# Writing a chunk mask into PSUM with VectorE instead of adding it with a TensorE matmul

## The chip, the cores and the metric

One Trainium2 chip, one of its cores. The metric is the device time of one execution, in microseconds (us).

## The reference

Two layers of a streaming encoder trunk over 1024 tokens of width 1024. Each layer norms its input, projects it, runs three branches (a gated linear recurrence, latent attention with 6 heads, a spatial gating MLP), and adds the normed output projection back. The change touches the scores of the attention alone. It is causal by chunks of 64 tokens: a query sees every key of its own chunk and of the chunks before it.

```python
s = jnp.einsum('bqhd,bkhd->bhqk', qb, k).astype(jnp.float32) * scale
mask = k_chunk[None, :] <= q_chunk[:, None]      # chunk = position // 64
s = jnp.where(mask[None, None], s, -jnp.inf)
p = jax.nn.softmax(s, axis=-1).astype(v.dtype)
return jnp.einsum('bhqk,bkhd->bqhd', p, v)
```

## The kernel before

All heavy products run on TensorE in a split form: each operand is kept as a rounded high part and a remainder, and `mm3` (L125 to L128) issues three matmuls for one product. The engines are written as one program; a scheduler orders each engine's instructions at build time from its own model of their durations, so a change in one operation can move others on every engine. At run time each engine executes its list in order, and a wait of one instruction holds all that stand behind it.

Each layer goes through these stages: the recurrent branch (`group`, `conv`, `lru_steps`), the spatial gating branch, the latents, the attention weights, the attention, and the output projection. The attention runs over 24 units per layer (6 heads x 4 pairs of 128-query blocks). For unit n the program emits `prepare(n + 4)` (queries and keys), `scores(n + 2)` and `mixv(n)`. So scores are made two units before they are used.

`scores` (from L884) makes two rows of scores per unit, one per 128-query block i, each over its (i + 1) x 128 keys. A row lies in PSUM in one of two buffers, `pw0` and `pw1`, each of two banks. The work of one row goes: `mm3` into the buffer, the mask, a row maximum on VectorE (L921), the exponential on ScalarE (L923, which also sums), a reciprocal on VectorE (L924), the scaling on GpSimd (L925). The buffer comes free when the exponential has read it. `mixv` then transposes the probabilities on TensorE (L945), splits them with ScalarE and VectorE or GpSimd (L365, L366), multiplies them with the values (L954), and combines the halves (L962, L963, L966).

The mask is needed in one 64x64 corner of a row: queries 0 to 63 of the block against keys 64 to 127 of the same block. Before the change the row's last `mm3` group is left open, and one more matmul closes it: `mask_a` (one partition, 128 columns, bf16: 64 ones, 64 zeros) times `mask_b` (one partition, 64 columns, bf16: -1e30). It adds -1e30 to the corner. The two tiles are set by three small memsets on VectorE at the start (L153 to L155). There are 2 layers x 24 units x 2 rows = 96 such matmuls, each with a weight load of its own.

At the program's start the prediction also speaks of `load_pre_gain` (L195, L197: a DMA, a transpose on TensorE), `load_x` (L183), the pre-norm (L327 on ScalarE, L133 to L142 and L338 on VectorE), the splitting of the transposed input (`turn_pair`, L349, L355, L356) and the convolution (L444 to L449), which reads the projected input out of `pw0` and `pw1`.

Of the kernel before, what the change touches and what calls it, by code (L numbers as in the profile page):

```python
# [9 lines left out]
BF16 = mybir.dt.bfloat16  # L10
# [9 lines left out]
EPS = 1e-6  # L20
# [17 lines left out]
NR, NF, NH = 33, 7, 3  # L38
# which of these run on VectorE rather than on GpSimd
W_ON_V = (C_U, C_GC)  # L40
Q_ON_V = ((0, 0), (0, 1), (1, 1), (4, 0))
Y_ON_V = (2, 4, 5, 6, 8, 9, 13, 14, 16, 19, 20, 21, 23)
WO_ON_V = (1, 4, 5)
# units of attention after which a token tile's share of the other branches is projected
EARLY = (20, 22)


class Slots:
    """A fixed set of buffers, handed out in the order in which they were given back."""

# [25 lines left out]
    def lend(self, t):  # L76
        """Add a buffer that is free for a while."""
        self.retired = [r for r in self.retired if r is not t]
        self.free_list.append(t)

    def retire(self, t):
        """No longer hand out a lent buffer."""
        self.retired.append(t)
        self.free_list = [r for r in self.free_list if r is not t]
# [5 lines left out]
def trunk_kernel(tc, A, out):  # L90
# [39 lines left out]
    def rsqrt(ms, n, out=None):  # L130
        """1 / sqrt(ms + EPS); times -8192 when `out` isn't given."""
        x, y, u = SM(n), SM(n), SM(n)
        V.tensor_scalar(out=x, in0=ms, scalar1=EPS, scalar2=None, op0=ALU.add)  # L133
        V.tensor_scalar(out=y.bitcast(I32), in0=x.bitcast(I32), scalar1=-0.5,
                        scalar2=float(0x5F3759DF), op0=ALU.mult, op1=ALU.add)
        for c in (3.0, 12.0, 768.0):
            if n == 1:
                V.scalar_tensor_tensor(out=u, in0=y, scalar=x, in1=y, op0=ALU.mult, op1=ALU.mult)  # L138
            else:
                V.tensor_tensor(out=u, in0=y, in1=y, op=ALU.mult)  # L140
                V.tensor_tensor(out=u, in0=u, in1=x, op=ALU.mult)
            V.scalar_tensor_tensor(out=y, in0=u, scalar=c, in1=y, op0=ALU.subtract, op1=ALU.mult)  # L142
        if out is not None:
            V.tensor_scalar(out=out, in0=y, scalar1=RSQ, scalar2=None, op0=ALU.mult)
        return y
# [4 lines left out]
    V.memset(ones, 1.0)  # L150
    mask_a = cst.tile([1, 128], BF16, name="mask_a")
    mask_b = cst.tile([1, 64], BF16, name="mask_b")
    V.memset(mask_a, 0.0)  # L153
    V.memset(mask_a[:, 0:64], 1.0)
    V.memset(mask_b, -1e30)  # L155
    Y = cst.tile([128, 8, T], F32, name="Y")
# [44 lines left out]
    def load_params():  # L201
        # per-channel parameters, transposed so that channels lie on partitions
        prow = HS.take((128, 128))
# [23 lines left out]
    def softplus_consts():  # L227
        V.tensor_scalar(out=hb, in0=par[:, 30:42], scalar1=0.5, scalar2=None, op0=ALU.mult)
        lam = par[:, 42:48]
        n = 6  # L230
        ab, kf, r, p, e, z, w = [SM(n) for _ in range(7)]
        # -|lam| = k ln2 + r
        V.tensor_scalar(out=ab, in0=lam, scalar1=-1.0, scalar2=None, op0=ALU.mult)
# [14 lines left out]
        V.tensor_tensor(out=e, in0=e, in1=p, op=ALU.mult)  # L248
        # log1p(e) = 2 atanh(e / (2 + e))
        V.tensor_scalar(out=z, in0=e, scalar1=2.0, scalar2=None, op0=ALU.add)  # L250
# [6 lines left out]
        V.scalar_tensor_tensor(out=p, in0=p, scalar=1.0, in1=z, op0=ALU.add, op1=ALU.mult)  # L257
        # softplus(-lam) = max(-lam, 0) + log1p(exp(-|lam|))
        V.tensor_scalar(out=k2, in0=lam, scalar1=-1.0, scalar2=0.0, op0=ALU.mult, op1=ALU.max)
# [58 lines left out]

    # ---------------------------------------------------------------- pieces
    def row_rsqrt(xs, cols=((0, 1024),), order=lambda i: i):  # L320
        """-8192 / rms of the rows of each of xs."""
        n = len(xs) * len(cols)
# [18 lines left out]
    def turn_pair(l, xn, hT, pair, slots):  # L341
        """Two token blocks of the normed input, turned and split in two parts."""
        half, o = pair // 2, (pair % 2) * 256
# [24 lines left out]
    class W:  # L368
        """Columns c0..c0+n of w_in, `per` row blocks to a buffer, split in two parts."""

# [28 lines left out]
    def feat(ps, hT, w, m, half, ts=slice(0, 512)):  # L399
        """[128 features, 512 tokens] of the input projection."""  # L400
        for k in range(8):
# [5 lines left out]
    def toks(hT, w, t, n, kind="P1"):  # L407
        """[128 tokens, n features] of the input projection."""
        ps = bank(kind)
# [7 lines left out]
    def gate_in(ps, yf, half):  # L417
        """Y[yf] = twice the silu of the projected gate."""
        th = HS.take((128, 512))
# [35 lines left out]
    def lru_steps(l, f, xc, gw):  # L455
        """The recurrence of channel block f as a list of pieces to emit."""
        c = l * 3 + f
# [62 lines left out]
    def stats(f0, n, ms, t0, width, eng, kind):  # L520
        """Mean square over n channel blocks for tokens t0..t0+512, onto partitions."""
        sq = []
# [14 lines left out]

    # ---------------------------------------------------------------- layers
    for r in yrow:
# [19 lines left out]
    for l in range(DEPTH):  # L559
        # ---- recurrent branch  # L560
        xc, last, gw = {}, [], []

        def group(g, half):
            pss = [bank("PF") for m in range(2)]
            if g == 0:
                # by pairs of token blocks, as they come
                for p in range(2):
# [46 lines left out]

        # ---- spatial gating branch
        for r in yrow[3:5]:
# [122 lines left out]

        # ---- latent attention: latents  # L740
        w = wl
# [49 lines left out]

        # ---- attention weights, norm gains folded in
        uqs, uq = [], []
# [30 lines left out]

        # ---- attention
        vs, vt, qs, kbs = {}, [], {}, {0: kb}
# [65 lines left out]
        def scores(h, j):  # L892
# [8 lines left out]
            for i in (2 * j, 2 * j + 1):  # L901
# [3 lines left out]
                ps = bank("P2") if j >= 2 else pw[:, (i % 2) * 512:(i % 2 + 1) * 512]  # L905
                # two equal pieces where the second would be too narrow for the full rate
                step = n // 2 if n == 640 else 512
                for c0 in range(0, n, step):
                    w = max(256, min(step, n - c0))
                    diag = c0 <= i * 128 < c0 + step  # L910
                    o0 = c0 // step * 512
                    mm3(ps[:, o0:o0 + w], sh, sl, kh[:, c0:c0 + w], kl[:, c0:c0 + w], True, not diag)
                    if diag:
                        d0 = o0 + i * 128 - c0 + 64
                        PE.matmul(ps[:, d0:d0 + 64], lhsT=mask_a, rhs=mask_b, start=False, stop=True)  # L915
                if step < 512:
# [16 lines left out]
        def mixv(h, j):  # L933
# [3 lines left out]
            for b0 in range(0, nb, 2):  # L937
                ps = bank("PT")
                pv = ps.rearrange("p (b q) -> p b q", b=2)
                end = b0 == nb - 2  # L940
                # the last key block comes first: the earlier query block doesn't see it
                for c, b in ((0, b0 + 1), (1, b0)):
# [92 lines left out]

        # ---- attention gate
        assert all(FS.idle(r) for r in yrow[5:])
# [38 lines left out]

        # ---- output projection, post-norm, residual, next pre-norm
        src = A["x"][0] if l == 0 else x1_dram
# [67 lines left out]
```

## Time and profile before

| what | value |
|---|---|
| time, median of 3 runs | 951.25 us (947.28 to 952.79) |
| span of the profiled execution | 948.6 us |
| TensorE (PE) busy | 899.4 us, 95% |
| VectorE (DVE) busy | 700.4 us, 74% |
| ScalarE (ACT) busy | 515.5 us, 54% |
| GpSimd (POOL) busy | 315.8 us, 33% |
| granted TensorE clock, mean | 0.984 of full |

The page gives no time of the profiled execution other than its span, from its first to its last instruction; this span lies inside the spread of the three times. The busy time of TensorE comes from modelled ends of pipelined matmuls; so for TensorE the distance from one matmul's start to the next one's tells more than the duration of one. The masks are issued in two stretches, from 252.4 to about 390 us in the first layer and from about 714 to 854.7 us in the second.

### The profile page before, as it was taken

The page shows a single profiled execution, that of the slowest core. Times are in us where ns is not written, and L with a number is a line of the kernel's source. Part 1 is how long each engine was busy: PE and PEld are TensorE (multiplying, and loading weights), DVE is VectorE, ACT ScalarE, POOL GpSimd, SP SyncE. Part 2 cuts the span into 40 slices and gives each one's busy share as a digit, 9 for nine tenths or more (in the row PEclk, how much of TensorE's full clock was granted, in tenths as well). Part 3 has the DMA queues.
Part 4 walks back from the last instruction along what each step waited for, and adds up shares of the span by engine and source line. Part 5 has one row for each costly group of instructions (what it writes and reads, how often), then busy time and mean ns, then how long its engine had stood idle before and what let it go on. Part 6 is the DMA issues. An engine that isn't in the chain of part 4 may idle for free. (4 is left out here: it accounts for less than half of the span.)

```text
span 948.6 us, 14005 instructions
## 1 busy us (share of the span) xinstructions
PE 899.4 (95%) x5078; PEld 775.8 (82%) x5078; DVE 700.4 (74%) x1645; ACT 515.5 (54%) x1026; POOL 315.8 (33%) x292
## 2 busy tenths in 40 slices
PE   4799999999999998998988999999999999899996
PEld 4698889998888877877887888899888888688785
DVE  6856976687588987588886498466857889857854
ACT  7346733346677886344444385323466778754312
POOL 2320013122156576353542000322103467655622
PEclk9899999999999999999999999999999999989999
DMA  7201410111000211022323032100100012201322
GB/s 269 52 24 44 120 31 1 41 39 32 1 1 23 89 45 45 26 86 98 122 92 97 1 114 65 38 18 23 48 1 1 1 46 67 67 23 46 123 99 89
DMA packets 35865, 53.39 MB, mean 56 GB/s; under 512 B 7800, under 2 KB 25812, under 8 KB 35796
## 3 DMA queue, kind: packets, MB, share of 16 engines
q1 hardware_dynamic: 35796, 52.50, 17.2%
q8 instruction: 40, 0.66, 0.3%
q14 instruction: 29, 0.24, 0.1%
HBM read 44.10 MB, written 8.39 MB: 55 GB/s over the span
## 5 line engine op out<-in xcount | busy, mean ns | idle before, releaser
L126 PE MATMUL pw<-R,R 128*128 128x512 f32 (+1 forms) x704 | 260.5, 371 | 13.8 <-ACT F L987 6.4
L127 PE MATMUL pw<-R,R 128*128 128x512 f32 (+1 forms) x704 | 253.3, 360 | 1.1 <-DVE R L356 1.1
L128 PE MATMUL pw<-R,R 128*128 128x512 f32 (+1 forms) x704 | 252.2, 359 | 0.7 <-POOL R L366 0.7
L126 PE MATMUL pa<-R,R 128*128 128x512 f32 (+3 forms) x540 | 188.6, 351 | 2.2 <-ACT F L768 2.2
L127 PE MATMUL pa<-R,R 128*128 128x512 f32 (+3 forms) x540 | 186.8, 346 | 0.0
L128 PE MATMUL pa<-R,R 128*128 128x512 f32 (+3 forms) x540 | 186.3, 346 | 0.0
L126 PEld LDWEIGHTS pw<-R,R 128*128 128x128 f32 x704 | 134.5, 191 | 34.3 <-ACT F L987 7.7
L128 PEld LDWEIGHTS pw<-R,R 128*128 128x128 f32 x704 | 134.2, 191 | 19.8 <-POOL R L366 1.1
L127 PEld LDWEIGHTS pw<-R,R 128*128 128x128 f32 x704 | 134.8, 192 | 18.6 <-DVE R L356 1.3
L385 POOL TENSOR_TENSOR R<-F,R 128x1024 fp32r<-128x1024 f32 (+1 forms) x22 | 49.3, 2256 | 190.8 <-ACT R L384 190.8
L925 POOL TENSOR_SCALAR F<-F,ring 128x128 f32<-128x128 f32 (+3 forms) x96 | 74.3, 776 | 114.6 <-DVE ring L924 109.2
L126 PEld LDWEIGHTS pa<-R,R 128*128 128x128 f32 x540 | 102.3, 190 | 12.3 <-ACT F L768 2.7
L128 PEld LDWEIGHTS pa<-R,R 128*128 128x128 f32 x540 | 102.3, 190 | 10.1
L127 PEld LDWEIGHTS pa<-R,R 128*128 128x128 f32 x540 | 102.4, 190 | 8.8
L921 DVE TENSOR_REDUCE ring<-pw 128x1 f32<-128x128 f32 (+3 forms) x96 | 71.9, 751 | 21.4 <-PE pw L915 20.4
L366 DVE TENSOR_TENSOR R<-pa,R 128x512 fp32r<-128x512 f32 (+1 forms) x120 | 73.8, 630 | 12.4 <-ACT R L365 11.4
L954 PE MATMUL pa<-R,R 128*128 128x256 f32 x480 | 77.9, 300 | 4.7 <-DVE H L963 4.5
L365 ACT ACTIVATE R<-pa 128x512 fp32r<-128x512 f32 (+1 forms) x120 | 64.4, 554 | 31.2 <-PE pa L945 25.3
L923 ACT ACTIVATE F<-pw,ring 128x128 f32<-128x128 f32 (+3 forms) x96 | 71.0, 740 | 13.9 <-DVE ring L921 13.2
L954 PEld LDWEIGHTS pa<-R,R 128*128 128x128 f32 x480 | 65.2, 195 | 7.8 <-DVE H L963 4.7
L945 PE MATMUL pa<-ident,F 128*128 128x128 f32 x432 | 67.4, 282 | 2.5 <-POOL R L366 1.5
L327 ACT ACTIVATE H<-F 128x1024 bf16<-128x1024 f32 (+2 forms) x33 | 31.4, 953 | 69.8 <-DVE F L1099 31.7
(276 smaller groups left out, 1400.3 us busy)
## 6 DMA issues: line engine op xcount, KB each, us to landing
F<-in_w_in SPq DMA_DIRECT2D x24, 512.0 KB, 3.8
F<-in_w_out SPq DMA_DIRECT2D x16, 512.0 KB, 3.6
F<-in_x SPq DMA_DIRECT2D x13, 512.0 KB, 3.5
F<-x SPq DMA_DIRECT2D x8, 512.0 KB, 4.3
x<-F SPq DMA_DIRECT2D x7, 512.0 KB, 3.0
out_y<-F SPq DMA_DIRECT2D x7, 512.0 KB
Y<-in_w_in SPq DMA_DIRECT2D x6, 512.0 KB, 3.5
F<-in_w_in SPq DMA_DIRECT2D x6, 352.0 KB, 3.0
```

Source lines behind the costliest of these rows:

```text
L126: PE.matmul(ps, lhsT=sh, rhs=mh, start=start, stop=False)
L127: PE.matmul(ps, lhsT=sh, rhs=ml, start=False, stop=False)
L128: PE.matmul(ps, lhsT=sl, rhs=mh, start=False, stop=stop)
L327: order(S_.activation(q.bitcast(BF16)[:, c], xs[i % len(xs)].rearrange("p a b -> p (a b)")[:, c], AF.Square, scale=1.0 / 32, accum_out=ms[ ...
L365: S_.activation(h, src, AF.Copy)
L366: (eng or G).tensor_tensor(out=lo, in0=src, in1=h.bitcast(F32), op=ALU.subtract)
L385: self.eng.tensor_tensor(out=lo, in0=st, in1=h.bitcast(F32), op=ALU.subtract)
L921: V.tensor_reduce(out=mx, in_=sv, axis=AX.XY, op=ALU.max, negate=True)
L923: S_.activation(p[:, 0:n].rearrange("p (a b) -> p a b", a=sv.shape[1]), sv, AF.Exp, bias=mx, accum_out=sm)
L925: G.tensor_scalar(out=p[:, 0:n], in0=p[:, 0:n], scalar1=rs, scalar2=1.0, op0=ALU.mult, op1=ALU.mult)
L945: PE.transpose(pv[:, c, i * 128:(i + 1) * 128], p[i][:, b * 128:(b + 1) * 128], ident)
L954: PE.matmul(o, lhsT=sv, rhs=pt[:, part, c * 256:(c + 1) * 256], start=(b == 0 and part == 0), stop=(b == nb - 1 and part == 1))
```

## The change

The mask tiles and their memsets go. The row's last `mm3` group closes itself, and VectorE writes -1e30 over the corner, 64 partitions by 64 columns of PSUM, before it takes the row maximum. The corner's scores are overwritten where they were added to. The program also loses its comments and docstrings. In the changed file the lines up to L150 keep their numbers, and those behind lie 5 lower, so the memset is L910 and the row maximum L916.

```diff
-    mask_a = cst.tile([1, 128], BF16, name="mask_a")
-    mask_b = cst.tile([1, 64], BF16, name="mask_b")
-    V.memset(mask_a, 0.0)
-    V.memset(mask_a[:, 0:64], 1.0)
-    V.memset(mask_b, -1e30)
...
                     w = max(256, min(step, n - c0))
-                    diag = c0 <= i * 128 < c0 + step
                     o0 = c0 // step * 512
-                    mm3(ps[:, o0:o0 + w], sh, sl, kh[:, c0:c0 + w], kl[:, c0:c0 + w], True, not diag)
-                    if diag:
+                    mm3(ps[:, o0:o0 + w], sh, sl, kh[:, c0:c0 + w], kl[:, c0:c0 + w], True, True)
+                    if c0 <= i * 128 < c0 + step:
+
                         d0 = o0 + i * 128 - c0 + 64
-                        PE.matmul(ps[:, d0:d0 + 64], lhsT=mask_a, rhs=mask_b, start=False, stop=True)
+                        V.memset(ps[0:64, d0:d0 + 64], -1e30)
```

The scheduler then orders the program anew. The lists differ in the two attention stretches and their surroundings and in the first 60 us or so; three places matter below. Names in the rows: `pw` and `pa` are PSUM tiles, F, H, R, Y and ring are SBUF tiles, and the number behind a name tells tiles apart (SBUF numbers are 5 lower after the change).

VectorE's list in the first layer's attention, before:

```order
L921 TENSOR_REDUCE ring<-pw_63 128x1
L366 TENSOR_TENSOR R_126<-pa_66,R_126 128x384
L366 TENSOR_TENSOR R_125<-pa_65,R_125 128x512
L963 SCALAR_TENSOR_TENSOR H_143<-pa_68,H_143 64x256
L881 TENSOR_TENSOR H_141<-pa_67,MQ 128x512
L924 RECIPROCAL ring<-ring 128x1 x2
L921 TENSOR_REDUCE ring<-pw_64 128x1
L366 TENSOR_TENSOR R_103<-F_138,R_105 128x1024
```

and after:

```order
L910 MEMSET pw_63 64x64
L958 SCALAR_TENSOR_TENSOR H_138<-pa_68,H_138 64x256
L876 TENSOR_TENSOR H_136<-pa_67,MQ 128x512
L361 TENSOR_TENSOR R_98<-F_133,R_100 128x1024
L916 TENSOR_REDUCE ring<-pw_63 128x1
L919 RECIPROCAL ring<-ring 128x1
```

The row maximum of the same row stood ahead of L963 (`mixv`), L881 (`queries`) and the 1024-wide remainder L366; now the memset stands ahead of these three and the maximum behind them. Over the whole list 27 of the 96 memsets have the maximum right behind them, 39 have one instruction between, 16 two and 14 three.

VectorE's list near 36 us, where the convolution reads the first projected blocks out of `pw0_63` and `pw1_64`, before:

```order
L449 SCALAR_TENSOR_TENSOR Y_82<-pw0_63,par_84,Y_82 128x510
L244 SCALAR_TENSOR_TENSOR ring_69<-ring_69 128x6
L446 COPY tails_99<-pw1_64 128x3
L449 SCALAR_TENSOR_TENSOR Y_82<-pw1_64,par_84,Y_82 128x511
L449 SCALAR_TENSOR_TENSOR Y_82<-pw0_63,par_84,Y_82 128x509
L245 TENSOR_SCALAR ring_69<-ring_69 128x6
L356 SCALAR_TENSOR_TENSOR R17_118<-pa2_67,pg_90,R16_117 128x256
L356 SCALAR_TENSOR_TENSOR R19_120<-pa3_68,pg_90,R18_119 128x256
```

and after:

```order
L444 SCALAR_TENSOR_TENSOR Y_77<-pw1_64,par_79,Y_77 128x511
L444 SCALAR_TENSOR_TENSOR Y_77<-pw0_63,par_79,Y_77 128x510
L239 SCALAR_TENSOR_TENSOR ring_69<-ring_69 128x6
L351 SCALAR_TENSOR_TENSOR R17_113<-pa2_67,pg_85,R16_112 128x256
L351 SCALAR_TENSOR_TENSOR R19_115<-pa3_68,pg_85,R18_114 128x256
L444 SCALAR_TENSOR_TENSOR Y_77<-pw1_64,par_79,Y_77 128x510
L351 SCALAR_TENSOR_TENSOR R21_117<-pa0_65,pg_85,R20_116 128x256
L351 SCALAR_TENSOR_TENSOR R23_119<-pa1_66,pg_85,R22_118 128x256
L444 SCALAR_TENSOR_TENSOR Y_77<-pw0_63,par_79,Y_77 128x509
L240 TENSOR_SCALAR ring_69<-ring_69 128x6
```

The last read of `pw0` (the 509-wide one) stood ahead of the four remainders of `turn_pair` and of the 510-wide read of `pw1`; now it stands behind these five. In both lists TensorE's next matmul writes `pw0`.

The queue of DMA issues (SP) at the program's start, before:

```order
L183 DMA F_134<-in_x 128x1024
L183 DMA F_135<-in_x 128x1024
L195 DMA H_141<-in_pre_norm_g 16x128
L375 DMA F_136<-in_w_in 128x4x256
L375 DMA F_137<-in_w_in 128x4x256
```

and after:

```order
L178 DMA F_129<-in_x 128x1024
L190 DMA H_136<-in_pre_norm_g 16x128
L178 DMA F_130<-in_x 128x1024
L370 DMA F_131<-in_w_in 128x4x256
L370 DMA F_132<-in_w_in 128x4x256
```

The load of the pre-norm gains and the load of the second token block have changed places.

## Rows read from the trace of the kernel before

**Rows 1.** The page, busy time of an engine, its share of the span and its instructions.
```profile
PE 899.4 (95%) x5078; PEld 775.8 (82%) x5078; DVE 700.4 (74%) x1645; ACT 515.5 (54%) x1026; POOL 315.8 (33%) x292
```

**Rows 2.** Busy time of each engine in stretches of the two attention stages. Columns: stretch, its length, then for PE, PEld (weight loads), DVE, ACT and POOL the busy us and the instructions, the granted TensorE clock, DMA share, GB/s.
```profile
240.00:260.00 20.00, 20.00 (x100) 16.66 (x99) 12.69 (x32) 11.51 (x30) 2.38 (x6) 1.00 0.00 1
260.00:360.00 100.00, 98.27 (x623) 81.39 (x622) 86.94 (x175) 79.15 (x172) 61.53 (x75) 1.00 0.13 43
360.00:400.00 40.00, 37.36 (x210) 32.18 (x210) 25.20 (x52) 20.46 (x40) 17.45 (x21) 0.96 0.08 27
700.00:720.00 20.00, 20.00 (x92) 16.42 (x91) 8.79 (x17) 12.57 (x20) 1.53 (x4) 1.00 0.00 0
720.00:820.00 100.00, 99.87 (x628) 83.47 (x627) 86.32 (x181) 78.16 (x176) 57.88 (x74) 1.00 0.11 38
820.00:860.00 40.00, 36.42 (x203) 30.87 (x202) 26.85 (x50) 23.48 (x48) 21.66 (x24) 0.91 0.08 27
```

**Rows 3.** The same view of shorter stretches: the one in which VectorE is fullest, and one behind a stall of TensorE.
```profile
320.00:340.00 20.00, 19.87 (x124) 16.17 (x123) 18.76 (x36) 18.66 (x38) 14.64 (x15) 1.00 0.24 80
...
364.60:368.00 3.40, 3.40 (x16) 3.21 (x15) 2.16 (x6) 2.25 (x5) 3.40 (x4) 0.50 0.02 5
```

**Rows 4.** The same view of the mask matmul's line (L915) alone, stretches as in rows 2; columns: stretch, length, PE busy (count), PEld busy (count), clock, DMA share, GB/s.
```profile
240.00:260.00 20.00, 0.99 (x5) 0.46 (x5) 1.00 0.00 1
260.00:360.00 100.00, 7.72 (x39) 3.53 (x39) 1.00 0.13 43
360.00:400.00 40.00, 0.79 (x4) 0.36 (x4) 0.96 0.08 27
700.00:720.00 20.00, 0.40 (x2) 0.18 (x2) 1.00 0.00 0
720.00:820.00 100.00, 7.72 (x39) 3.54 (x39) 1.00 0.11 38
820.00:860.00 40.00, 1.39 (x7) 0.64 (x7) 0.91 0.08 27
```

**Rows 5.** TensorE in order of time around two masks of the first layer. Columns: start (us), duration (us), engine, line, operation, tiles, array size, shape, count.
```profile
342.17 0.27 PE L127 MATMUL pw<-R,R 128*128 128x256 f32 x1
342.28 0.28 PE L128 MATMUL pw<-R,R 128*128 128x256 f32 x1
342.50 0.20 PE L915 MATMUL pw<-mask_b,mask_a 1*128 1x64 bf16 x1
342.62 0.50 PE L126 MATMUL pa<-R,R 128*128 128x512 f32 x1
342.96 0.40 PE L127 MATMUL pa<-R,R 128*128 128x512 f32 x1
343.19 0.39 PE L128 MATMUL pa<-R,R 128*128 128x512 f32 x1
...
349.59 0.40 PE L128 MATMUL pw<-R,R 128*128 128x512 f32 x1
349.92 0.20 PE L915 MATMUL pw<-mask_b,mask_a 1*128 1x64 bf16 x1
350.05 0.33 PE L945 MATMUL pa<-ident,F 128*128 128x128 f32 x1
```

**Rows 6.** Who waited for whom, longest first: for the first row TensorE from 250 to 360 us, for the others VectorE from 260 to 360 us and from 720 to 820 us. Columns: waiter, releaser, us in total, times, longest us.
```profile
PE pw L126 <- ACT F L923: 0.5, 1, 0.5
...
DVE ring L921 <- PE pw L915: 4.4, 9, 1.5
...
DVE ring L921 <- PE pw L915: 6.0, 12, 1.5
```

**Rows 7.** VectorE, operations near to the new one: a 64-column memset in SBUF and two small operations of which the second needs the first (in order of time), and the row maximum over 128 columns of PSUM (a group: count, busy us, mean ns, idle before it).
```profile
0.84 0.11 DVE L153 MEMSET mask_a<- 1x64 uint32 x1
...
7.49 0.17 DVE L133 TENSOR_SCALAR ring<-ring 128x2 f32<-128x2 f32 x1 [1.00 <-ACT H L327]
7.70 0.17 DVE L134 TENSOR_SCALAR ring<-ring 128x2 int32<-128x2 int32 x1
...
L921 DVE TENSOR_REDUCE ring<-pw 128x1 f32<-128x128 f32 x12 | 3.4, 282 | 2.9 <-PE pw L915 2.7
```

**Rows 8.** Groups of VectorE by line and shape: the three operations that now stand between a memset and its row maximum at the place shown.
```profile
L963 DVE SCALAR_TENSOR_TENSOR H<-pa,H 64x256 f32<-64x256 f32 x48 | 20.1, 419 | 10.2 <-ACT H L962 9.2
L881 DVE TENSOR_TENSOR H<-pa,MQ 128x512 f32<-128x512 f32 x24 | 16.4, 685 | 4.5 <-PE pa L879 3.3 <-POOL F L925 0.6 <-issue 0.2
L366 DVE TENSOR_TENSOR R<-F,R 128x1024 fp32r<-128x1024 f32 x7 | 9.3, 1324 | 5.1 <-PE pw L127 3.4 <-PE pa L128 1.5
```

**Rows 9.** The start, in order of time: the issue of the gains' load, the second square of the pre-norm, the five operations of VectorE near 40 us, and TensorE's first matmul behind them.
```profile
1.65 0.42 SPq L195 DMA_DIRECT2D H<-in_pre_norm_g  x1
...
6.31 1.06 ACT L327 ACTIVATE H<-F 128x1024 bf16<-128x1024 f32 x1 [0.94 <-PE pa L197]
...
39.28 0.87 DVE L356 SCALAR_TENSOR_TENSOR R<-pa,pg,R 128x256 fp32r<-128x256 f32 x2
40.07 0.74 DVE L449 SCALAR_TENSOR_TENSOR Y<-pw,par,Y 128x510 f32<-128x510 f32 x1
40.72 0.86 DVE L356 SCALAR_TENSOR_TENSOR R<-pa,pg,R 128x256 fp32r<-128x256 f32 x2
...
39.44 0.77 PE L126 MATMUL pw<-R,R 128*128 128x512 f32 x1 [6.14 <-DVE ring L245]
```

## The prediction, made before the changed kernel ran

> **What bounds the kernel now.** I read the share of busy time first, then the same busy times by stretches, because a share over the whole span mixes stages. TensorE is busy 95% of the span, VectorE 74% [rows 1]. In the two dense stretches of the attention, 260 to 360 us and 720 to 820 us, TensorE is busy 98.27 and 99.87 of 100 us, at a granted clock of 1.00 (2.4 GHz), and VectorE 86.94 and 86.32 [rows 2]. A busy TensorE need not be a limiting one, so I looked at who waits: TensorE waits 0.5 us in all for a score buffer [rows 6], and the only large wait of VectorE is for the mask matmul, 4.4 and 6.0 us [rows 6]. So the dense stretches run at TensorE's pace, with VectorE close behind: in its fullest 20 us it is busy 18.76, or 0.94 [rows 3]. The whole prediction rests on this narrow distance. TensorE loses work and VectorE gains some, so the second engine may take over before the first has given all its time back.
>
> **The change part by part.**
>
> *Mask matmuls removed.* There are 96: 39 in each dense stretch, 5 and 2 ahead of them, 4 and 7 behind [rows 4]. Their own 0.20 us in the records is not their price; I take the distance between starts with and without one. In the first example the 256-wide L128 starts at 342.28 and the second 512-wide matmul behind the mask at 342.96, so 0.68 us. Without a mask a 256-wide step takes 0.11 (342.17 to 342.28) and a 512-wide one 0.23 (342.96 to 343.19), together 0.34. The mask costs 0.34 us here [rows 5]: half ahead of its own start or in it, the rest in a slow first matmul behind it. In the second example 0.46 us pass from the 512-wide L128 to the first transpose, where 0.23 would do; the mask costs 0.23 [rows 5]. I take the middle, 0.29 us: 27.8 us in all, 11.3 in each dense stretch. The ends are 22 and 33 us.
>
> The Trainium skill ("TensorE: Matmul & The Clock Gate", Back-to-back issue gap) gives a matmul of up to 64 columns about 60 cycles, 25 ns. By it the 96 masks are worth 2.4 us, and the change next to nothing. The trace disagrees: even from the mask's start to the next start there are 0.12 us.
>
> *Memsets added.* 96 on VectorE, 64 columns, to PSUM. No row shows this. From below: the memset of 64 columns to SBUF takes 0.11 us [rows 7]. From above: a row maximum over 128 columns read from PSUM takes 0.28 us [rows 7], with twice the columns and a read. The maximum must wait for the memset's result; in the chain of small operations a needed result adds 0.04 us (0.17 us long, the next starts 0.21 later [rows 7]). I take 0.11 + 0.04 = 0.15 us, near the memset row because nothing is read. Its wait for TensorE is the one that the row maximum had, so it is not a new one. The ends are 0.11 and 0.28.
>
> The Trainium skill ("VectorE: DVE Perf Modes", The TRN2 errata) gives an operation that reads PSUM 120 cycles and one per column at 0.96 GHz; for 64 columns that is 0.19 us, an estimate from that page. With it the dense stretches would gain some 3.4 us less than in my sum, 944 us in all. No row here shows a write to PSUM by VectorE.
>
> *The balance in the dense stretches.* TensorE would need 100 - 11.3 = 88.7 us. VectorE would need 86.94 + 39 x 0.15 = 92.8 and 86.32 + 5.9 = 92.2, so VectorE ends last. It cannot be busy all the time while it works hand in hand with three engines. I take a share of 0.97, between the 0.94 that it has shown while it did not set the pace and 1.00. The stretches become 95.7 and 95.0 us, a gain of 4.3 and 5.0. At 0.94 the gain is 1.3 and 1.9, at 1.00 it is 7.2 and 7.8.
>
> *The edges.* From 240 to 260 and from 700 to 720 us VectorE is busy 12.69 and 8.79 of 20 us [rows 2], so the 7 masks there give back their whole price, 2.0 us. From 360 to 400 and 820 to 860 us TensorE already idles 2.6 and 3.6 us at the end of the softmax chain, and the clock sits partly at 0.50 (1.2 GHz) behind a stall [rows 2, 3]; of 11 masks worth 3.2 us I count 1.0. Both ends there, 0 and 3.2, lie inside the range.
>
> *The start.* The scheduler moved two things there that have nothing to do with masks. TensorE stood idle 6.14 us until VectorE had read `pw0` for the last time, and went on at 39.44 [rows 9]. That read now has five more operations ahead of it. They took 0.79 (39.28 to 40.07), 0.65 (40.07 to 40.72) and again 0.79 us [rows 9]: 2.2 us later, all of it on the path, since TensorE is the busy one from there to the attention. Against it, the gains' load is issued one place earlier, 0.42 us [rows 9]; the second square of the pre-norm waited for the transpose of these gains [rows 9], and the chain to the first matmuls starts from it. I count -0.4 us; if the token block, now issued later, decides there instead, +0.4. The three mask memsets at the start cost nothing: VectorE waits for that square anyway. Together +1.8 us.
>
> *Sum.* Gains 4.3 + 5.0 + 2.0 + 1.0 = 12.3, less 1.8: 10.5 us. The profiled execution spans 948.6 us, 2.6 below the median of the runs and inside their spread. I take the gain off the median: 951.25 - 10.5 = 940.8, say **941 us**. With the memset at 0.11 or the share at 1.00 it would be 937 or 935; at 0.28 about 951, at 0.94 about 947.
>
> **The rivals.**
>
> *TensorE keeps the pace.* The scheduler may pack VectorE's list so that its load does not matter; many of its operations overlap the tail of the one before, and the other waits of VectorE are short. Then all of 27.8 us comes back: 951.25 - 27.8 + 1.8 = 925 us (920 to 931 with the ends of the price). Against it stands the 0.94 in rows 3, where ScalarE too is busy 18.66 of 20.
>
> *VectorE takes up everything.* With 0.28 us a memset VectorE needs 97.9 and 97.2 us, at 0.97 that is the old 100; only the edges gain, and the start takes that back: about 951 us, no change.
>
> *The mask was never worth more than its issue slot.* If the slow matmul behind it has another cause and the 0.12 us overlap what follows, TensorE is hardly relieved: between 949 and 953 us. That is what the skill's rule on the issue gap above comes to. Both examples in rows 5 speak against it.
>
> *Score buffers held longer, and the kernel slower.* The order shows a memset, then `mixv`'s combine, a query product and a 1024-wide remainder, then the row maximum. These three take 0.42 + 0.69 + 1.32 = 2.4 us [rows 8], by which that row's exponential comes later and its PSUM buffer comes free later. In 30 of the 96 rows two or three operations stand between. TensorE needs one of the two buffers for every row, and its list cannot pass a matmul that waits. Net of the start my sum holds 10.5 us; that is gone if each of the 30 rows holds TensorE by 0.35 us, a seventh of the 2.4. At 0.6 us each it is 18 us lost against 10.5 won: 959 us. For it: VectorE has no room to catch up, and a stall of TensorE is followed by a stretch at clock 0.50 [rows 3]. Against it: today TensorE waits only 0.5 us for a buffer [rows 6], and scores are made two units ahead.
>
> **How the numbers follow.** A measurement of this kernel can tell about 0.5% (4.8 us) from no change, so faster means below 946.5 and slower above 956. My forecast, VectorE taking over part of the way, has 0.45 (931 to 946 us). TensorE keeping the pace has 0.14, VectorE taking up everything 0.21, the cheap mask 0.04, held buffers 0.16. Faster: 0.45 + 0.14 = 0.59. Same: 0.25. Slower: 0.16. The range goes from 926, which leaves out half of the second case, to 958, which leaves out the greater part of the last.
>
> **What would show it.** Right: no L915 matmul and the first matmul behind a score row at its plain step; dense stretches of some 95 us with VectorE at 0.95 or more; TensorE now with scattered waits for VectorE or ScalarE; memset rows of 0.11 to 0.2 us; TensorE starting on the second group near 41.5 us instead of 39.44. The forecast is wrong if VectorE's share stays near 0.87 while the stretch shrinks by 11 us (the first rival), if memsets take 0.28 us or more with what waits behind them (the second), if the matmuls at the place of the mask move up by 0.1 us or less (the third), or if TensorE's waits for ScalarE's exponential (now 0.5 us) grow to 10 us and more (the last).

## The result, and the profile after

The changed kernel takes 961.73 us (median of 4 runs, 960.38 to 965.3) against 949.9 of the kernel before on the same chip: ratio 1.0126, interval 1.0093 to 1.0158. It is 1.3% slower where 1% faster was forecast, and 3.7 us outside the range. The profiled execution is the longest of the four (span 963.5 us). One of e2's five executions below took 4226.61 us at a mean clock of 0.197 and is left out of its time.

The page's busy line, to be read beside [rows 1]: TensorE has 12 us less to do, VectorE 17 more, and the span is 15 longer.

```profile
PE 887.0 (92%) x4982; PEld 775.8 (81%) x4982; DVE 717.0 (74%) x1738; ACT 515.1 (53%) x1026; POOL 311.5 (32%) x292
```

The stretches of [rows 2], columns as there:

```profile
240.00:260.00 20.00, 20.00 (x94) 16.96 (x93) 9.91 (x20) 12.38 (x21) 0.94 (x3) 1.00 0.00 0
260.00:360.00 100.00, 93.35 (x581) 80.77 (x579) 93.45 (x216) 76.26 (x173) 55.62 (x73) 0.98 0.12 38
360.00:400.00 40.00, 34.17 (x188) 30.00 (x186) 26.97 (x56) 24.73 (x50) 23.06 (x25) 0.91 0.08 27
720.00:820.00 100.00, 93.76 (x573) 81.59 (x572) 90.56 (x213) 75.36 (x171) 51.05 (x70) 0.98 0.09 27
```

Without its 39 masks TensorE issued 584 matmuls from 260 to 360 us before; now it issues 581, and 573 instead of 589 in the second stretch (the stretches lie some 6 and 9 us earlier in the program now). So the freed time brought no more work through there. VectorE stands at 0.93 and 0.91, neither engine is full.

Who kept TensorE waiting (waiter, releaser, us in total, times, longest us; whole span, changed kernel):

```profile
PE pa L344 <- DVE F L333: 12.0, 2, 11.5
PE pa L940 <- DVE R L361: 11.5, 10, 2.8
PE pw L126 <- DVE ring L240: 9.9, 1, 9.9
PE pw L126 <- ACT F L982: 9.2, 4, 5.2
...
PE pw L126 <- ACT F L918: 3.2, 9, 0.5
```

The same waits in the kernel before:

```profile
PE pa L349 <- DVE F L338: 6.8, 3, 4.2
PE pw L126 <- ACT F L987: 6.4, 4, 2.9
PE pw L126 <- DVE ring L245: 6.1, 1, 6.1
...
PE pa L945 <- DVE R L366: 1.0, 1, 1.0
```

The wait for the exponential (L918), on which my slower case rested, is 3.2 us in all (0.5 before). What has grown are the waits of the transposes (L940) for VectorE's remainders, the two at the start (the first transposes, L344, and the second group, L126 behind L240), and the longest one for the projection's copy on ScalarE (L982). The memset's group (count, busy us, mean ns, idle ahead of it; who released VectorE) shows 0.112 us:

```profile
L910 DVE MEMSET pw<- 64x64 f32 x96 | 10.7, 112 | 9.2 <-PE pw L128 8.2
```

The start, answering to [rows 9]. The second square waits for the token block now (1.6 us later), two of VectorE's small operations take 2.3 us each, beside two splits on GpSimd, and the second group starts at 45.95 us instead of 39.44:

```profile
7.88 1.06 ACT L322 ACTIVATE H<-F 128x1024 bf16<-128x1024 f32 x1 [2.65 <-DMA F<-in_x]
...
10.38 4.65 POOL L380 TENSOR_TENSOR R<-F,R 128x1024 fp32r<-128x1024 f32 x2 [9.07 <-ACT R L379]
10.45 2.29 DVE L142 SCALAR_TENSOR_TENSOR ring<-ring 128x2 f32<-128x2 f32 x1
12.78 2.27 DVE L140 TENSOR_TENSOR ring<-ring 128x2 f32<-128x2 f32 x1
...
45.95 0.76 PE L126 MATMUL pw<-R,R 128*128 128x512 f32 x1 [9.87 <-DVE ring L240]
```

To find the place of a loss I took landmarks from the timelines (the first, 9th and last of the 48 row maxima of a layer, the last value product of `mixv`, the last matmul of `stats`). Lengths in us; e1, e3 and e10 are explained below:

| from - to | before | after | e1 | e3 | e10 |
|---|---|---|---|---|---|
| start - first row maximum, layer 0 | 252.7 | 258.7 | 255.4 | 255.5 | 255.3 |
| - 9th row maximum | 16.2 | 17.0 | 16.2 | 17.0 | 15.9 |
| - last row maximum | 119.2 | 116.2 | 118.1 | 114.9 | 112.2 |
| - last `mixv` product | 17.4 | 22.8 | 17.0 | 22.8 | 17.2 |
| - first row maximum, layer 1 | 308.8 | 309.2 | 307.3 | 307.9 | 307.0 |
| - 9th row maximum | 21.5 | 19.9 | 20.0 | 19.9 | 19.2 |
| - last row maximum | 119.2 | 115.9 | 116.5 | 116.1 | 113.7 |
| - last `mixv` product | 22.7 | 26.9 | 22.4 | 26.9 | 22.6 |
| - last `stats` matmul | 10.9 | 18.3 | 10.9 | 18.5 | 10.8 |
| - end | 60.0 | 58.6 | 59.9 | 58.6 | 60.0 |

The dense part between the 9th and the last row maximum is 3 us shorter per layer, which looks like the forecast. It isn't: in the changed kernel TensorE issues 67 instead of 50 `mm3` matmuls of the output projection behind the last row maximum (91 instead of 74 in layer 1), 17 x 0.23 = 3.9 us of work that was only moved there. The loss is 6.0 us ahead of the attention and, net of that moved work, in its tails and behind them (against e1 the dense part of layer 1 loses too, see e8).

### The profile page after: what moved, and what is told of

The parts are those of the page before. It is cut to its first block, busy times and chain, and to the rows that moved or that the text cites. A ratio compares the mean times of both kernels' runs of the same rounds, so it can differ in the third digit from the quotient of the medians.

```text
span 963.5 us, 13911 instructions
## 1 busy us (share of the span) xinstructions
PE 887.0 (92%) x4982; PEld 775.8 (81%) x4982; DVE 717.0 (74%) x1738; ACT 515.1 (53%) x1026; POOL 311.5 (32%) x292
## 3 DMA queue, kind: packets, MB, share of 16 engines
q1 hardware_dynamic: 35796, 52.50, 17.2%
## 5 line engine op out<-in xcount | busy, mean ns | idle before, releaser
L126 PE MATMUL pw<-R,R 128*128 128x512 f32 (+1 forms) x704 | 260.6, 372 | 23.4 <-DVE ring L240 9.9
L126 PE MATMUL pa<-R,R 128*128 128x512 f32 (+3 forms) x540 | 187.1, 349 | 2.2 <-ACT F L763 2.2
L126 PEld LDWEIGHTS pw<-R,R 128*128 128x128 f32 x704 | 135.2, 193 | 49.4 <-ACT F L982 10.5
L126 PEld LDWEIGHTS pa<-R,R 128*128 128x128 f32 x540 | 102.3, 190 | 11.8 <-ACT F L763 2.7
L918 ACT ACTIVATE F<-pw,ring 128x128 f32<-128x128 f32 (+3 forms) x96 | 71.0, 741 | 27.4 <-DVE ring L916 19.8
L940 PE MATMUL pa<-ident,F 128*128 128x128 f32 x432 | 67.8, 282 | 13.0 <-DVE R L361 11.5
L916 DVE TENSOR_REDUCE ring<-pw 128x1 f32<-128x128 f32 (+3 forms) x96 | 71.7, 749 | 1.3
L360 ACT ACTIVATE R<-pa 128x512 fp32r<-128x512 f32 (+1 forms) x120 | 62.3, 553 | 16.8 <-PE pa L940 14.1
```

Of the source, the lines that this page charges most:

```text
L126: PE.matmul(ps, lhsT=sh, rhs=mh, start=start, stop=False)
L360: S_.activation(h, src, AF.Copy)
L916: V.tensor_reduce(out=mx, in_=sv, axis=AX.XY, op=ALU.max, negate=True)
L918: S_.activation(p[:, 0:n].rearrange("p (a b) -> p a b", a=sv.shape[1]), sv, AF.Exp, bias=mx, accum_out=sm)
L940: PE.transpose(pv[:, c, i * 128:(i + 1) * 128], p[i][:, b * 128:(b + 1) * 128], ident)
```

## The experiments

**The tool: order held fast.** The change did two things, an operation and a new order. To have one without the other I wrote each engine's list into the kernel as a permutation and gave each instruction an edge behind its predecessor, which orders the issue and is meant to add no wait:

```diff
+def pin(tc):
...
+    for e, s in PIN.items():
+        at = np.frombuffer(zlib.decompress(base64.b85decode(s)), np.uint16)
+        for a, b in zip(at[:-1], at[1:]):
+            tc.add_manual_dep(by[e][b], by[e][a].name, mybir.DependencyInfo(
+                mybir.DependencyClass.NoSync, mybir.DependencyReason.DATA), reason="pin")
...
+    pin(tc)
```

Its 24 lines stand ahead, so in e1 and e3 line numbers are 24 above those of the changed kernel: `mm3` is L150 to L152, the projection's copy L1006, the one-column steps of the norm L162 and L166. The lists of the two kernels differ in three blocks (start, attention of layer 0, attention of layer 1 with its tail) and agree between them, so blocks can be mixed. All but the last experiment were timed in 5 rounds beside the kernel before (its medians 950.9 to 951.8). The kernel before with its own order held was not run; e11, which is that with 96 more matmuls, lies 1.0 us above it, so the holding itself changes little.

**e1: the memset, in the order of before.** Edit: changed kernel, `PIN` = order of before.

> The memset as in the change, but every engine's instructions pinned to the order of the kernel before (each memset directly ahead of its row maximum on VectorE, the mask matmuls simply missing on TensorE). Theory O (the change lost its time by the new order, at the start and in the attention): faster than before, 938 to 946 us, first group's second half at 39 to 41 us as before. Rival V (the memset itself costs it, because VectorE sets the attention's pace and every 0.11 us there delays a row maximum): no faster than before, 950 to 956 us.

945.53 us, ratio 0.994 (0.9918 to 0.9963). Theory O: the operation alone makes the kernel 5.5 us *faster*.

**e2: the matmul, in the new order.** Edit: kernel before, `PIN` = order of the changed kernel, the three small memsets later on VectorE.

> The converse: the mask matmul of the kernel before, but all other instructions pinned to the order of the changed kernel. Theory O: at least as slow as the changed kernel, 960 to 975 us, since order and matmuls both cost. Rival V: only the start's 6 us are lost, 954 to 958 us.

974.8 us (four executions), ratio 1.025 (1.0222 to 1.0277). The order costs about 24 us where nothing else is changed.

**e3: the changed kernel with the old start.**

> The changed kernel with its own order, only the start (TensorE's first 192, VectorE's first 136, ScalarE's first 46 instructions, SP's queue) pinned to the order of before. If the later start is a matter of order alone: the row maxima of layer 0 begin at about 252.7 us instead of 258.7, and the time falls by 5 to 7 us to 954 to 957 us. Rival (the start is late for what stands in the instruction stream, not for its order, or the lateness is absorbed later): less than 2 us gained, 960 to 963 us.

959.63 us, ratio 1.0091 (1.0071 to 1.011): 2.1 us better than the change, between what I expected and the rival, and the two intervals overlap. The row maxima begin at 255.5 us, not at 252.7, mostly because the two long rows stay (see e6, e17). Against e1 only the order of the two attentions differs: 14.1 us.

**e4: no mask at all, order of before.** Edit: the memset and its condition out.

> Neither matmul nor memset: the mask is left out of the computation, all else in the order of before. This shows what the 96 matmuls alone are worth where nothing takes their place. Theory O with VectorE near its limit: 930 to 941 us. If TensorE's time in the attention is fully covered by VectorE and the row maxima: 947 to 951 us. If all 27.8 us come back: 922 to 926 us.

932.71 us, ratio 0.9808 (0.9784 to 0.9833). So the 96 matmuls are worth 18.3 us, 0.19 each, and the memsets in their place cost 12.8 (e1 less e4), 0.13 each. The dense stretches of e1, then of e4 (columns as in [rows 2]):

```profile
260.00:360.00 100.00, 92.82 (x592) 80.46 (x591) 95.10 (x221) 80.26 (x177) 61.41 (x77) 1.00 0.14 43
720.00:820.00 100.00, 94.35 (x605) 82.39 (x604) 95.73 (x230) 81.60 (x184) 61.02 (x76) 1.00 0.14 43
```

```profile
260.00:360.00 100.00, 93.27 (x605) 82.38 (x604) 94.08 (x189) 83.85 (x182) 65.14 (x80) 0.99 0.13 43
715.00:815.00 100.00, 93.49 (x612) 83.12 (x611) 94.00 (x195) 85.47 (x190) 63.74 (x79) 1.00 0.14 43
```

VectorE at 0.95 and 0.96 in e1, as forecast, and matmuls brought through: 592 and 605 in e1 against 584 and 589 before, 605 and 612 with no mask.

**e6: do the dead memsets at the start matter?** Edit: e1 with the two mask tiles and their three memsets back.

> As e1 (memset, order of before), with the three small memsets of the two mask tiles kept at the places at the start where they stood before, though nothing reads the tiles now. Two VectorE rows of 2.2 us stood behind the first pre-norm in the kernel before and in front of it in e1. Theory S (what stands ahead in VectorE's stream sets where these long rows fall): first transposes at about 10.5 us instead of 15.3, second half of the first group near 39.4 instead of 41.7, time 942 to 944 us. Rival (they fall by something else): first transposes stay at 15, time 945 to 947 us.

944.62 us (0.9911 to 0.9946); transposes at 15.0 us. Theory S falls.

**e7: new order in layer 0 alone.**

> As e1, but the attention of layer 0 alone in the order of the changed kernel. Against e1 the new order cost 3 us by the end of layer 0's attention and 11 more in layer 1 (e3). Theory O: 948 to 950 us, all of it in place at layer 1's first row maximum. Rival (the order of layer 0 triggers the loss of layer 1, through buffers and queues left in another state): 954 to 960 us.

947.52 us (0.995 to 0.9986), 2.0 above e1, just under what O expected and with overlapping intervals; in the profile 3.8 us behind e1 at layer 1's first row maximum and 3.5 at the end. The loss stays in its layer, as O has it.

**e8: new order, tail of before.** Edit: from TensorE's instruction 4421, VectorE's 1504, ScalarE's 772, GpSimd's 260 on, the order of before.

> As e3 (memset, new order in both attentions, old start), but from about 840 us on, the tail of layer 1's attention, every engine in the order of before. Theory T (the new order's tail leaves TensorE without work for the 5.2 us in which ScalarE's projection copy waits, and the clock falls behind it): that gap shrinks to about 1.3 us, no 0.5 clock there, 951 to 954 us. Rival (the gap comes from the later arrival of the whole attention, not from the order in the tail): 957 to 960 us.

955.3 us (1.0031 to 1.0061), 4.3 us better than e3. The mechanism is T's, the size is half. The tail of layer 1 in e3, in order of time: a tile's norm runs on VectorE in one-column operations (L162, L166), which take 0.8 to 1.5 us while GpSimd runs eight splits (L385), where they take 0.16 to 0.22 us with GpSimd idle (897.4 to 898.4 us). Then the residual (L1118) frees the buffer that ScalarE's copy (L1006) takes next, by the program (the copy starts 0.09 us behind it in both kernels; the view names no releaser), and that copy frees TensorE's:

```profile
880.04 11.50 POOL L385 TENSOR_TENSOR R<-Y,R 128x640 fp32r<-128x640 f32 x8 [2.17 <-PE pa L973]
...
882.64 1.50 DVE L162 SCALAR_TENSOR_TENSOR ring<-ring 128x1 f32<-128x1 f32 x1
...
884.17 1.50 DVE L166 SCALAR_TENSOR_TENSOR ring<-ring 128x1 f32<-128x1 f32 x1
...
888.22 2.46 DVE L1118 SCALAR_TENSOR_TENSOR F<-F,ring,F 128x1024 f32<-128x1024 f32 x1
...
890.77 1.11 ACT L1006 ACTIVATE F<-pw,ra 128x1024 f32<-128x1024 f32 x1 [7.08 <-issue]
...
891.94 0.80 PE L150 MATMUL pw<-R,R 128*128 128x512 f32 x1 [5.17 <-ACT F L1006]
```

The same chain in e1:

```profile
869.56 11.71 POOL L385 TENSOR_TENSOR R<-Y,R 128x640 fp32r<-128x640 f32 x8
...
876.76 1.94 DVE L1118 SCALAR_TENSOR_TENSOR F<-F,ring,F 128x1024 f32<-128x1024 f32 x1
878.79 1.11 ACT L1006 ACTIVATE F<-pw,ra 128x1024 f32<-128x1024 f32 x1 [4.00 <-PE pw L152]
879.96 0.50 PE L150 MATMUL pw<-R,R 128*128 128x512 f32 x1 [1.29 <-ACT F L1006]
```

The chain is nearly as long in e1: 10.3 us from the first split to the end of the copy, 11.8 in e3. But there GpSimd's splits begin 3.6 us before the last `mixv` product (873.2), in e3 1.3 us before it (881.3), so TensorE has run out of other work. It stands 5.17 us instead of 1.29, and the granted clock falls to 0.50 (1.2 GHz) within that stall and stays there to 897 us (e3, columns as in [rows 2]):

```profile
880.00:887.00 7.00, 6.77 (x35) 5.46 (x34) 6.32 (x7) 3.64 (x8) 6.96 (x5) 1.00 0.00 0
890.50:897.00 6.50, 5.06 (x12) 4.05 (x13) 5.60 (x9) 3.62 (x6) 5.06 (x4) 0.50 0.46 161
897.10:899.00 1.90, 1.90 (x11) 1.55 (x11) 1.67 (x6) 0.00 (x0) 0.27 (x1) 1.00 0.00 0
```

In e8 the gap is 1.29 us again and the clock from 874 to 894 us is 1.00. What is left of layer 1's loss in e8's profile lies between the 9th and the last row maximum, 123.1 us against 116.5 in e1. Columns as in [rows 2], e8, then e1:

```profile
739.30:862.30 123.00, 108.78 (x659) 94.32 (x659) 103.33 (x226) 85.34 (x182) 67.13 (x84) 0.96 0.13 39
```

```profile
734.00:850.50 116.50, 107.31 (x665) 93.43 (x664) 102.07 (x230) 86.91 (x184) 69.43 (x85) 0.97 0.13 42
```

TensorE idles 14.2 us there instead of 9.2, at a slightly lower mean clock; its longest wait in total there is that of the transposes for VectorE's remainders, 5.8 us instead of 3.5. (This profile is of the longest of e8's ten executions, 2.0 us above their median.)

**e9: each corner written twice, order of before.**

```diff
                         V.memset(ps[0:64, d0:d0 + 64], -1e30)
+                        V.memset(ps[0:64, d0:d0 + 64], -1e30)
```

> As e1, but each corner is written twice, so that VectorE has 96 more memsets of 0.11 us, 10.8 us in all. Theory V2 (VectorE sets the attention's pace once the matmuls are gone): 955 to 959 us. If VectorE has slack in most rows: 946 to 951 us.

958.49 us (1.0058 to 1.0092): 13.0 us for 96 more. None, one and two memsets give 932.7, 945.5 and 958.5: a straight line at 0.13 us each, the row's 0.112 and a little more. V2's price holds, nothing covers VectorE's operation once the matmul is gone. But VectorE is busy only 0.92 and 0.91 of the dense stretches of e9, so the price does not show a VectorE that is full.

**e10: ScalarE writes the corner, order of before.**

```diff
-                        V.memset(ps[0:64, d0:d0 + 64], -1e30)
...
                 p = FS.take((128, 1024)) if j >= 2 else pair[:, i % 2]
+                S_.activation(ps[0:64, d0:d0 + 64], mask_c, AF.Copy)
```

> Order of before; the corner is written by ScalarE, as a copy of a constant tile straight ahead of the exponential and behind the row maximum (the maximum then covers the unmasked corner too, which is an upper bound all the same). Neither TensorE nor VectorE has the mask. Theory (VectorE pays 0.13 us a corner in e1 and ScalarE has slack in the attention): between e4 (932.7, no mask) and e1 (945.5), 934 to 941 us. Rival (96 copies of some 0.25 us delay the exponentials, whose score buffers TensorE waits for): 945 to 956 us.

936.09 us, ratio 0.9836 (0.9813 to 0.9858): 25.6 us below the change, and the best but for e4, which leaves the mask out. The copies take 0.21 us, longer than the memset, on the engine that had room; VectorE keeps 0.91:

```profile
L943 ACT ACTIVATE pw<-mask_c 64x64 f32<-64x64 f32 x96 | 20.5, 213 | 10.5 <-DVE ring L941 10.3
```

Here the row maximum stands ahead of the mask and no longer waits for it. How much of the gain is that, and how much the change of engine, was not measured.

**e11: the mask matmul twice, order of before.**

```diff
+                        PE.matmul(ps[:, d0:d0 + 64], lhsT=mask_a, rhs=mask_b, start=False, stop=False)
                         PE.matmul(ps[:, d0:d0 + 64], lhsT=mask_a, rhs=mask_b, start=False, stop=True)
```

> The kernel before in its own order with each mask matmul issued twice. Taking the 96 matmuls away brought 18.3 us (e4), 0.19 each. If TensorE sets the pace in before, the second set costs its whole price of 0.23 to 0.34 each: 973 to 983 us. If VectorE shares the limit already in before, about the same 18 us or less: 960 to 970 us.

952.79 us, ratio 1.0019 (1.0003 to 1.0034). Both of my cases fail: the second set costs 1.0 us by the medians (952.79 less 951.82). TensorE in order of time around one pair:

```profile
302.06 0.31 PE L151 MATMUL pw<-R,R 128*128 128x320 f32 x1
302.20 0.31 PE L152 MATMUL pw<-R,R 128*128 128x320 f32 x1
302.45 0.20 PE L939 MATMUL pw<-mask_b,mask_a 1*128 1x64 bf16 x1
302.48 0.19 PE L940 MATMUL pw<-mask_b,mask_a 1*128 1x64 bf16 x1
302.60 0.33 PE L970 MATMUL pa<-ident,F 128*128 128x128 f32 x1
```

0.25 us into the first mask, 0.03 to the second, 0.12 out. The price is in the passage into and out of the mask, and a second one in between is nearly free (0.03 us at each width of the score matmul). The Trainium skill ("TensorE: Matmul & The Clock Gate", Back-to-back issue gap) gives about 25 ns for such a matmul: the median of 39 ns between the starts of a pair comes near it, the first matmul's 0.19 us does not.

**e12: no mask, new attention order, old start.** Edit: e3 without the memset.

> Neither matmul nor memset (the mask is left out of the computation), start in the order of before, both attentions in the order of the changed kernel; to e3 as e4 is to e1. If the new order's loss is independent of the memset: 959.6 less 12.8, 945 to 949 us. If the new order loses because VectorE is full and only then: much of the 14 us comes back, 934 to 941 us.

952.9 us, ratio 1.0015 (0.9999 to 1.0031): 20.2 us above e4, and above both of the times expected. The new order loses even with no memset in it, more than with it (14.1), so neither the memset nor the load that it adds to VectorE is needed for the loss.

**e13: matmul and memset, order of before.**

> The kernel before in its own order with the memset added behind the mask matmul, so both operations. If VectorE's memset costs its 0.13 us whatever TensorE does: 962 to 965 us. If it is covered while TensorE still sets the pace: 951 to 957 us. The start also shows whether VectorE's two long rows stay behind the first pre-norm (transposes at 10.5 us) when VectorE's program is longer but TensorE's is that of before.

956.93 us (1.0039 to 1.0074), 5.1 above before: while TensorE still pays for its matmuls, more than half of the memset's price is covered. Transposes at 14.9 us.

**e14: new order, each memset directly ahead of its row maximum.** Edit: e3 with the memsets moved down in `PIN`.

> As e3 (memset, start of before, new order in both attentions: 959.6 us), but every memset moved down on VectorE to stand directly ahead of its own row maximum, so that no operation lies between. Rival H (the prediction's slower case: the maximum comes later than its memset by what stands between, and the score buffer is held): 945 to 954 us. Theory O (the loss is in the rest of the order, since it is there with no memset at all, e12): 957 to 962 us.

961.42 us (1.0088 to 1.0138), no better than e3. Held buffers (H) fall: the loss stays with nothing between the two.

**e15: the mask tiles in 4 bytes, order of before.** Edit: `BF16` to `F32R` in both tiles.

> The kernel before in its own order, with the two mask tiles in the 4-byte type of the score operands instead of bf16; the mask matmul is otherwise the same. The first mask matmul is worth 0.19 us and a second one behind it 0.03 at most (e11). If the price lies in the change of type and back: 936 to 944 us. If it lies in the change of weights or of the array's shape (1 row instead of 128): 948 to 953 us. If the 4-byte type streams slower: up to 965 us.

959.63 us (1.0061 to 1.0109), 8.7 slower than before. Its row takes 292 ns, the bf16 one 198. So taking away the change of type brought nothing back; since the 4-byte row is itself 0.09 us longer, the type's own share stays open, and whether the rest is the change of weights or of the array's shape, e11 and e15 don't tell.

**e16: e10 with the scheduler's own order.** Edit: e10 without `PIN`.

> As e10 (ScalarE writes the corner ahead of the exponential: 936.1 us), but with the order left to the scheduler as in the two kernels given. If its order costs about what it did with the memset (16 us) or without any mask (20 us): 950 to 958 us. If it happens to find a good one: 930 to 940 us.

959.73 us, ratio 1.0081 (1.0053 to 1.0109): 23.6 us above e10 and just above what I expected. Here too the scheduler's own order takes back more than the edit brings. The tail of layer 1 is again slow: 10.7 us behind before at the last `stats` matmul.

**e17: the kernel before once more.**

> The kernel before, unchanged, for a second profile of it. If the place of the two long VectorE rows at the start belongs to the program: behind the first pre-norm operations again, first transposes at 10.5 us. If it changes from run to run: transposes at about 15 us, as in every rearranged kernel but e2.

One run, 948.94 us. The long rows stand on both pre-norm operations this time (two operations of 2.91 and 2.84 us), transposes at 12.7 us, and the second group at 41.0 instead of 39.4. VectorE and GpSimd in order of time, now and then in the first profile of the kernel before:

```profile
9.54 0.16 DVE L142 SCALAR_TENSOR_TENSOR ring<-ring 128x2 f32<-128x2 f32 x1
9.73 5.67 DVE L338 TENSOR_SCALAR F<-F,ring 128x1024 f32<-128x1024 f32 x2
9.74 5.11 POOL L385 TENSOR_TENSOR R<-F,R 128x1024 fp32r<-128x1024 f32 x2 [8.44 <-ACT R L384]
...
15.32 0.15 DVE L133 TENSOR_SCALAR ring<-ring 128x2 f32<-128x2 f32 x1
```

```profile
9.47 0.16 DVE L142 SCALAR_TENSOR_TENSOR ring<-ring 128x2 f32<-128x2 f32 x1
9.66 3.52 DVE L338 TENSOR_SCALAR F<-F,ring 128x1024 f32<-128x1024 f32 x2
9.78 5.62 POOL L385 TENSOR_TENSOR R<-F,R 128x1024 fp32r<-128x1024 f32 x2 [8.47 <-ACT R L384]
```

The long rows are the ones that run beside GpSimd's first two splits, as in the changed kernel, where the splits start at 10.38 and 12.69 us and the long rows at 10.45 and 12.78. In the 18 profiles here the first split starts between 8.85 and 10.38 us. Where it starts no earlier than the last small operation of the pre-norm (this profile and the first one, e2, e8), the transposes start at 10.5 to 12.8 us, in all others at 14.7 to 16.3. So the place of the long rows changes from run to run of one program. With the start in the order of before, the second group begins 1.6 to 2.3 us behind the first profile's 39.4 in every other profile, and about that much of the start's difference between two profiles is chance.

## Why the prediction was wrong, point by point

**The order, the step that failed.** "The change part by part" priced an operation against an operation in a program that otherwise ran as before; of the new order it counted two moves at the start. With the order held (e1) the change is faster by 5.5 us, inside my range and on my side. The new order costs 16.2 us on top (961.7 less 945.5): 2.1 at the start (e3 against the change, not clear of their spread), 14.1 in the attentions. Of these, 2.0 by the medians (3.5 in the profile) lie in layer 0 (e7) and 4.3 in layer 1's tail (e8, shown by its gap and clock); the rest, about 7, lies in the dense part of layer 1 (123.1 us in e8 against 116.5 in e1), where TensorE idles 5 us more in pieces of 0.1 to 2.8 us, the largest part in front of transposes that wait for VectorE's remainders. Why these come later in the new order was not found, and it stays open. e2, e12 and e16 show that the order loses whatever writes the mask.

**The matmul's price, mis-sized.** I took 0.29 us, 27.8 in all; e4 gives 0.19, 18.3, below my lower end. In the dense stretches the next matmul behind a 256-wide last score matmul starts 0.34 us later with the mask and 0.12 without, behind a 512-wide one 0.46 and 0.23 (medians, before and e4): a price of 0.22 to 0.23, whatever follows. My second example showed it. The first, 0.34, has 0.10 more in a slow first matmul, which stands in the rows only where a query product follows, at 11 of the 96 places. Of the 22 us that these distances add up to the kernel gives back 18.3.

**The memset, right in sum.** Its row is 0.112 us, not 0.15, but on average 0.13 lies on the path (e4, e1, e9): 12.8 us in all. My working put 39 x 0.15 / 0.97 = 6.0 us on the path in each dense stretch and nothing at the edges, 12.1. So of my gains of 12.3 us 5.5 came with the order held, and nearly all that is missing is what taking the matmuls away brings: 18.3 us (e4), where the same working without a memset gives 24.4.

**The balance, right in kind.** In the old order VectorE did take over, at 0.95 and 0.96 where I had 0.97, though e4 has 0.94 with no memset at all. More work came through by 592/584 and 605/589, 1.4 and 2.7 us in 100 instead of 4.3 and 5.0, as the smaller price of the matmul less the memset would have it: 39 x (0.19 - 0.13) = 2.3.

**The edges.** I counted +2.0 for the first masks; in the old order the first nine rows give 0.0 and 1.5 (16.2 to 16.2, 21.5 to 20.0). I counted +1.0 for the tails. In the old order they give 0.4 and 0.3 (17.4 to 17.0, 22.7 to 22.4); in the new one the stretch from last row maximum to last `stats` matmul is 11.6 us longer in layer 1, of which 3.9 is work moved there.

**The start.** +1.8 counted, +6.0 in the profile. The sentence that the token block could decide instead came true, with 1.6 us instead of 0.4. The later read of `pw0`, which I had at 2.2 us, is mis-sized too: TensorE's wait there is 9.8 to 9.9 us in the three profiles with the new start (the change, e2, e16) and 6.1 to 6.4 in all others, so 3.4 to 3.8. The rest is the long rows, about 2 us of which are chance (e17).

**The rivals.** TensorE keeping the pace and VectorE taking up everything both fail in e1. The cheap mask fails in e4, though it describes a second mask well (e11). Held buffers had the right sign, and with 959 us nearly the right time, but by luck: the wait for the exponential rose by 2.7 us, not 10, and e14 gains nothing.

## What to carry to other kernels

Where a scheduler orders the program anew, an edit has two effects, and the second can be the larger: price the operation with the order held fast, and read the difference of the two orders as a change of its own, above all at the tails, where a stall of TensorE was paid again at the lower clock (e3: 5.17 us, then 0.50 to 897 us). The order also decides which of VectorE's small operations run beside GpSimd's splits. A small operation belongs on the engine with room at that place, even if it takes longer there (e10: 0.21 us on ScalarE beat 0.11 on VectorE).

## What the runs showed of the hardware

- A one-row bf16 matmul between 4-byte ones moves the next start by 0.22 us at every width of the matmul ahead, 0.19 us in the kernel's time; a second one behind it by 0.03 (before, e4, e11).
- VectorE writes a 64x64 corner of PSUM in 0.112 us (all 96 alike).
- VectorE's one-column operations take 1.5 us instead of 0.16 to 0.22 while GpSimd runs splits of 1.57 us, one beside the other in turn (e3, 882 to 886 us). The Trainium skill ("Trainium Architecture — The Big Picture", What this means for kernel authors) names a port pair that VectorE and GpSimd share under an exclusive lock; these rows agree with it.
- In the 18 profiles, 861 of 11,340 of VectorE's operations of up to six columns into `ring` last over 0.4 us, and every one of them overlaps an operation of GpSimd. Not each one that overlaps is slow.
